# The decay exponents of an SSD scan move from VectorE to ScalarE, and the running sums get another layout in DRAM

## The chip, the cores and the metric

The kernel runs on one core of a Trainium2 chip. The metric is the device time of one execution in microseconds (us). Three executions of the kernel before took 1712.23, 1719.13 and 1721.5 us, so the median is 1719.13 us.

## The reference, cut to what matters

One layer is computed for a prompt of 1024 tokens and for 32 sample rows. It has dilated attention (12 heads), a Mamba-2 SSD scan (16 heads in two groups of 8) beside it, a common output projection and a feed-forward part with a convolution. The change is in the SSD scan of the prompt, which works on 8 chunks of 128 tokens:

```python
acum = jnp.cumsum(dtc * a.reshape(G, hpg), axis=2)
causal = jnp.tril(jnp.ones((q, q), bool))[:, :, None, None]
seg = acum[:, :, :, None] - acum[:, :, None, :]
decay = jnp.exp(jnp.where(causal, seg, -jnp.inf))
cb = jnp.einsum('bcign,bcjgn->bcijg', cc, bc)
y_intra = jnp.einsum('bcijg,bcijgh,bcjghp->bcighp', cb, decay, xdt)
```

`acum` is the running sum of dt * a inside a chunk. `a` is negative, so `seg` is zero or less where the mask is true. The kernel doesn't form minus infinity: it clamps `seg` at zero, takes the exponential, and has the mask in the factor `cb`.

## The kernel before, in words

Every product is made of three float32r products (a high and a low part of each operand). The main stream of TensorE is a list of weight chunks. A chunk has three units of 24 matmuls over 352 tokens each (L1037 to L1039, tile `p_mm`). After a unit its results are taken from PSUM on VectorE, the next chunk's weights are split (`wh` on ScalarE, `wl` on VectorE), and one tick of the side work follows.

The SSD scan is such side work: 16 steps, one for each pair of a group g and a chunk c. A step is a generator, `ssd_gen`, and a tick takes each running step one stage on. The stages are: transposes on TensorE; `xdt` and `cbm`; the decay (`M`, `Ab`, `xdw`); the products M * cbm on VectorE (L1271) and Ab * C on GpSimd (L1272); the matmuls into `p_sa` (L1280 with M, L1285 with Ab, L1287 with xdw); the evacuation on VectorE (`hn`, L1294 or L1296, and `XS`, L1300). `p_sa` has one buffer, so a step's matmuls wait until VectorE has evacuated the step before. For group 0 a new step starts every second tick, for group 1 at every tick. The order on each engine is that in which the program emits the instructions; no engine overtakes its own queue.

For each step the running sums of 8 heads and 128 tokens are loaded from the DRAM scratch `acscr` to all 128 partitions at once (`Ab`, three buffers in rotation; the load for the next step is issued on SyncE's DMA queue, SP, in the stage that takes the present one). In the kernel before `acscr` is stored as 16 heads by 1024 tokens, so a partition's 4 KB come as 8 pieces of 512 bytes. `M` has two buffers.

Of the kernel before, what the change touches and what calls it, by code (L numbers as in the profile page):

```python
# [11 lines left out]
F32 = mybir.dt.float32  # L12
# [7 lines left out]
D = 1024  # L20
S = 1024
# [18 lines left out]
def host_constants():  # L40
    """Arrays that depend on shapes alone: identity, masks and the ALiBi bias of each group."""
    f = np.float32
    c = {}
    i = np.arange(128)
    c["ident"] = np.eye(128, dtype=f)
    c["triu"] = (i[:, None] <= i[None, :]).astype(f)
    h = np.arange(1, NH + 1, dtype=f)
    slopes = np.exp2(f(-8.0) * h / f(NH)).astype(f).reshape(3, 4)
    for g in range(2):
        step = (i[:, None] + 128) - np.arange(256)[None, :]  # L50
        ok = (step >= 0) & (step <= 128)
        b = -slopes[g][None, :, None] * (step * DIL[g]).astype(f)[:, None, :]
        c[f"bias{g}"] = np.where(ok[:, None, :], b, f(NEG)).astype(f)
    step = i[:, None] - i[None, :]
    ok = (step >= 0) & (i[:, None] // 64 == i[None, :] // 64)
    b = -slopes[2][None, :, None] * (step * DIL[2]).astype(f)[:, None, :]
    c["bias2"] = np.where(ok[:, None, :], b, f(NEG)).astype(f)
    bs = np.full((128, 3, 9, 4, 4), NEG, f)
    c16 = i % 16
    for g in range(3):  # L60
        for u in range(U_S[g]):
            for t in range(4):
                if g == 0:
                    step = 128 + t - (9 * c16 + u)
                    ok = (step >= 0) & (step <= 128)
                elif u == U_S[g] - 1:
                    step = 0 * c16
                    ok = c16 == 15
                else:
                    n = U_S[g] - 1  # L70
                    step = 16 * n - n * c16 - u
                    ok = step >= 0
                bb = -slopes[g][None, :] * (step * DIL[g]).astype(f)[:, None]
                bs[:, g, u, t, :] = np.where(ok[:, None], bb, f(NEG))
    c["bias_s"] = bs.reshape(128, 3, 144)
    c["blk16"] = (i[:, None] // 16 == i[None, :] // 16).astype(f)
    c["bsel"] = (i[:, None] // 16 == np.arange(8)[None, :]).astype(f)
    j = np.arange(32)
    same = j[:, None] // 4 == j[None, :] // 4
    btri = (same & (j[:, None] <= j[None, :])).astype(f)  # L80
    pk = np.zeros((128, 256), f)
    pk[:32, 0:32] = btri
    pk[:32, 32:64] = same.astype(f)
    pk[:32, 64:192] = np.tile(btri, (1, 4))
    pk[:, 192:224] = (i[:, None] % 32 == j[None, :]).astype(f)
    for q in range(2):
        pk[:, 224 + q] = (q * 4 + i // 32 == (i % 32) // 4)
    pk[:96, 226:234] = (i[:96, None] % 32 // 4 == np.arange(8)[None, :])
    pk[:16, 234:242] = (np.arange(16)[:, None] // 2 == np.arange(8)[None, :])
    c["pack"] = pk  # L90
    c["par"] = (np.arange(16)[:, None] % 2 == i[None, :] // 64).astype(f)
    return c
# [24 lines left out]
def raw_ap(base, offset, dims):  # L117
# [3 lines left out]
# Buffers in SBUF: shape, type, number in rotation, first and last phase of use. A pair of types makes  # L121
# two views of the same bytes (what a DMA brings, and the rounded part that takes its place).
RAW = (F32, F32R)
BUFFERS = {
    # constants and small things
# [9 lines left out]
    # x, load  # L135
    "xh": ([128, K8, NT], F32R, 1, 0, 6), "xl": ([128, K8, NT], F32R, 1, 0, 6),
    "xt": ([128, D], F32, 4, 0, 0), "jk": ([128, D], F32, 1, 0, 0), "sx": ([128, 4, 128], F32, 2, 0, 0), "xr": ([128, 4, 128], F32, 4, 0, 0), "cst_in": ([128, 3, 128], F32, 1, 1, 1), "cst_g": ([8, 128], F32, 1, 0, 0),
    # q, k, v
# [4 lines left out]
    # attention of the prompt  # L143
# [7 lines left out]
    # attention of the sample rows  # L151
# [5 lines left out]
    # dt  # L157
# [3 lines left out]
    # weights with tokens moving  # L161
    "wl": ([128, D], RAW, 3, 2, 9), "wh": ([128, D], F32R, 2, 2, 9),
    # convolution, SSD, gate
# [12 lines left out]
    # w_out  # L176
# [6 lines left out]
    # feed-forward  # L183
# [6 lines left out]
class Memory:  # L190
    """Places the buffers: those whose phases are apart may share bytes."""
# [22 lines left out]
    @staticmethod  # L214
    def place(items, base, end):
        """Lowest free place for each item in turn; the place of each, or the first that found none."""
        placed, where = [], {}
        for n, (size, name, i, t0, t1) in enumerate(items):
            at = base
            for lo, hi in sorted((o, o + z) for o, z, a, b in placed if not (b < t0 or a > t1)):  # L220
                if at + size <= lo:
                    break
                at = max(at, hi)
            if at + size > end:
                return None, n
            placed.append((at, size, t0, t1))
            where[name, i] = at
        return where, None
# [14 lines left out]
class Side:  # L243
    """Work that runs between the units of the main stream: queues of generators, each advanced a
    stage at a time. A generator that yields True goes on before the next unit's results are taken
    (for what takes the results of its own products), otherwise after."""
# [40 lines left out]
def body(tc, A):  # L287
# [42 lines left out]
    acscr = dr.tile([16, S], F32, name="acscr")  # L330
    acsscr = dr.tile([16, NS], F32, name="acsscr")

# [51 lines left out]
    def rsqrt_mean(dst, src, n, cols):  # L384
        """dst = (src / n + eps) ^ -0.5, on the [P, cols] of both."""
        G.tensor_scalar(dst, src, 1.0 / n, EPS, op0=ALU.mult, op1=ALU.add)
        G.tensor_tensor(dst, dst, neghalf[: dst.shape[0], :cols], op=ALU.pow)
# [14 lines left out]
    def wq_load(sl):  # L402
        """Half slices of w_in for q, k or v of a group, to be split in two parts."""
# [106 lines left out]
    def states_in(sp, dst, nm, rows, per, nf):  # L510
        """A convolution's state of the sample rows, features on partitions."""
# [198 lines left out]
    def att_chain(g, at):  # L710
        """Tiles of a group, four of them under way; a tile's keys stay for the next one."""
        gens = [att_gen(g, i, at) for i in range(8)]
        return gens

# [1 line left out]
    # Partition 16*b + c holds the c-th part of the keys of row b of the batch; every partition does a  # L716
    # softmax of its own part, and the parts of all groups are put together at the end.
# [206 lines left out]
    def dt_gen():  # L924
# [9 lines left out]
        # softplus(x) = max(x, 0) + 2 atanh(e / (2 + e)), e = exp(-|x|)  # L934
# [44 lines left out]
        for q2 in range(2):  # L979
# [6 lines left out]
            SP.dma_start(acscr[:, q2 * 512:(q2 + 1) * 512], aT)  # L986
# [29 lines left out]
    def w_split(n, part, low):  # L1016
        """Half of a weight chunk in two parts: the high one, or the low one."""
# [13 lines left out]
    def fm_unit(ps, hl, moving, c0, k0, k1):  # L1031
        """ps[128 features, CH tokens] += (rows of a weight chunk)^T @ tokens, both in two parts."""
# [15 lines left out]
    def chunk(n, moving, evac, psum=p_mm, after=None, more=None, steps=(0, 2, 2, 2), hold=None, first=0):  # L1048
        """The three units of a weight chunk; the elementwise work of the chunk before runs between them.
        The first rows of all units may go ahead of the others."""  # L1050
# [49 lines left out]
    # ================= q, k, v =================  # L1100
    def group_end(g):
        """What waits for the last tile of a group to be in DRAM."""
# [16 lines left out]
    def samp_rows(g, w):  # L1119
        """What the rows of the sample group of k (w = 1) or v (w = 2) start."""  # L1120
# [52 lines left out]
    # ================= xBC: convolution, SSD =================  # L1173
# [58 lines left out]
    def ab_load():  # L1232
        """The sums of dt * a of the next chunk, the same on every partition."""
        if ab_order:
            g, c = ab_order.pop(0)
            Ab = R("Ab")
            SP.dma_start(Ab, raw_ap(acscr, g * 8 * S + c * 128, [[0, 128], [S, 8], [1, 128]]))
            decays[g, c] = Ab

    def ssd_gen(g, c):  # L1240
# [21 lines left out]
        for h in range(8):  # L1262
            V.tensor_scalar(M[:, h, :], Ab[:, h, :], acum[:, c, g * 8 + h:g * 8 + h + 1], 0.0, op0=ALU.subtract,  # L1263
                            op1=ALU.min)
        AC.activation(M, M, AF.Exp)
# [90 lines left out]
    def samp_ssd():  # L1356
# [5 lines left out]
        # three copies of the tokens, so that a product over 96 rows takes both parts of both operands  # L1362
# [67 lines left out]
        def state(c):  # L1430
            """The states of two heads: what they add to y, decay and new part."""
# [52 lines left out]
    # ================= z: gate =================  # L1484
# [67 lines left out]
    # ================= w_out =================  # L1552
# [6 lines left out]
    def rms_cols(src, dst, scr):  # L1559
        """Per token (sum over features of src / D + eps)^-0.5, the same on every partition of dst."""  # L1560
# [84 lines left out]
    # ================= feed-forward =================  # L1645
# [201 lines left out]
```

## Time and profile before

| | kernel before |
|---|---|
| device time, three executions | 1712.23, 1719.13, 1721.5 us |
| span of the profiled execution | 1718.4 us |
| TensorE (PE) busy | 1627.3 us, 95% |
| VectorE (DVE) busy | 1086.4 us, 63% |
| ScalarE (ACT) busy | 586.2 us, 34% |
| GpSimd (POOL) busy | 406.7 us, 24% |

The span is the time from the first to the last instruction of one profiled execution. The profile gives no separate device time for that execution; its span lies 0.7 us under the median of the three. The shares are means over the whole span, and the stages differ a good deal: the SSD steps lie between 521 and 702 us.

### The profile page before, as it was taken

Reading aid. Unit: us, or ns where it says so; the run is one execution under the profiler, and the core shown is the slowest. Engines: PE = TensorE matmul, PEld = TensorE weight load, DVE = VectorE, ACT = ScalarE, POOL = GpSimd, SP = SyncE. Lnnn points to the kernel's source line nnn. Section 1 sums busy time; section 2 is a strip of 40 time slices with the busy share of each in tenths; the row PEclk is TensorE's granted clock in tenths of the full one; section 3 lists DMA queues with packets and bytes.
Section 4 is the critical chain, followed back from the end, with each engine's and each line's share of the span. In section 5 each row is a group of like instructions: output and inputs, shape, how many; then the busy total and the mean of one; then the engine's idle time right before and its main releaser. Section 6 shows DMA issues by size and latency. Waiting matters only on the chain.

```text
span 1718.4 us, 27938 instructions
## 1 busy us (share of the span) xinstructions
PE 1627.3 (95%) x11167; PEld 1570.2 (91%) x11167; DVE 1086.4 (63%) x1921; ACT 586.2 (34%) x1062; POOL 406.7 (24%) x455
## 2 busy tenths in 40 slices
PE   6988997999998988989999999999999999999998
PEld 6877987889998877889999999999999999999998
DVE  6578877725568898666354555645547456465565
ACT  6424534525734544432232331221221222222121
POOL 6576556400013456531021100000000000000000
PEclk9999998999999998989999999999999999999999
DMA  7543565544355242455211211021120210211102
GB/s 242 145 155 113 168 194 161 148 130 119 79 152 142 59 89 63 143 160 164 66 41 47 92 50 51 25 75 38 37 63 14 75 50 26 63 47 41 51 1 103
DMA packets 193024, 158.16 MB, mean 92 GB/s; under 512 B 18802, under 2 KB 176010, under 8 KB 192895
## 3 DMA queue, kind: packets, MB, share of 16 engines
q1 hardware_dynamic: 192895, 156.38, 31.4%
q8 instruction: 88, 1.44, 0.3%
q14 instruction: 41, 0.34, 0.1%
HBM read 127.63 MB, written 34.68 MB: 94 GB/s over the span
## 4 chain that ended last, share of the span: by engine, by line
PE 75%; DVE 9%; DMA 7%; POOL 3%; issue 3%; ACT 2%; SPq 1%; DVEq 0%; ACTq 0%; POOLq 0%
PE p_up L1037 10%; PE p_up L1039 10%; PE p_up L1038 10%; PE p_mm L1037 6%; PE p_mm L1038 6%; PE p_mm L1039 6%; PE p_dn L1783 5%; PE p_dn L1781 5%; PE p_dn L1782 5%; DMA Ab<-acscr 2%; PE p_mm L554 2%; DVE sq L591 1%; PE p_mm L555 1%; PE p_mm L556 1%; DVE M L1263 1%
## 5 line engine op out<-in xcount | busy, mean ns | idle before, releaser
L1037 PE MATMUL p_up<-x2h,wh 128*128 128x352 f32 x1032 | 334.5, 324 | 0.0
L1039 PE MATMUL p_up<-x2h,wl 128*128 128x352 f32 x1032 | 333.4, 323 | 0.0
L1038 PE MATMUL p_up<-x2l,wh 128*128 128x352 f32 x1032 | 332.9, 323 | 0.0
L1691 DVE TENSOR_TENSOR fci<-p_up,rb 128x352 f32<-128x352 f32 x129 | 66.2, 513 | 238.7 <-PE p_up L1039 237.1
L1037 PEld LDWEIGHTS p_up<-x2h,wh 128*128 128x128 f32 x1032 | 194.1, 188 | 0.2
L1038 PEld LDWEIGHTS p_up<-x2l,wh 128*128 128x128 f32 x1032 | 193.8, 188 | 0.0
L1039 PEld LDWEIGHTS p_up<-x2h,wl 128*128 128x128 f32 x1032 | 193.8, 188 | 0.0
L1785 DVE TENSOR_TENSOR yacc<-yacc,p_dn 128x352 f32<-128x352 f32 x264 | 133.6, 519 | 75.5 <-PE p_dn L1783 75.5
L554 PE MATMUL p_mm<-wqh,xh 128*128 128x256 f32 (+1 forms) x576 | 171.0, 297 | 1.6 <-DVE sb L570 1.6
L1781 PE MATMUL p_dn<-gp,dh 128*128 128x352 f32 x528 | 172.3, 326 | 0.0
L1783 PE MATMUL p_dn<-gp,dl 128*128 128x352 f32 x528 | 171.3, 324 | 0.0
L1782 PE MATMUL p_dn<-gp,dh 128*128 128x352 f32 x528 | 171.0, 324 | 0.0
L556 PE MATMUL p_mm<-wqh,xl 128*128 128x256 f32 (+1 forms) x576 | 165.9, 288 | 0.9 <-POOL xl L461 0.7
L555 PE MATMUL p_mm<-wql,xh 128*128 128x256 f32 (+1 forms) x576 | 165.7, 288 | 0.0
L1037 PE MATMUL p_mm<-xh,wh 128*128 128x352 f32 x480 | 162.5, 338 | 0.0
L1039 PE MATMUL p_mm<-xh,wl 128*128 128x352 f32 x480 | 155.9, 325 | 1.5 <-DVE wl L1027 1.4
L1038 PE MATMUL p_mm<-xl,wh 128*128 128x352 f32 x480 | 156.2, 325 | 0.0
L1029 ACT CAST wh<-wl 128x512 fp32r<-128x512 f32 (+1 forms) x160 | 92.0, 607 | 112.8 <-PE p_up L1038 76.6
L1027 DVE TENSOR_TENSOR wl<-wl,wh 128x512 fp32r<-128x512 f32 (+1 forms) x160 | 120.0, 750 | 3.8 <-ACT wh L1029 3.7
L1709 DVE SCALAR_TENSOR_TENSOR facc<-fci,cw,facc 128x1072 f32<-128x1072 f32 x88 | 116.8, 1327 | 2.1 <-ACT facc L1701 2.0
L554 PEld LDWEIGHTS p_mm<-wqh,xh 128*128 128x128 f32 x576 | 112.5, 195 | 4.9 <-DVE sb L570 1.8
L556 PEld LDWEIGHTS p_mm<-wqh,xl 128*128 128x128 f32 x576 | 112.1, 195 | 1.5 <-POOL xl L461 1.5
(359 smaller groups left out, 3458.0 us busy)
## 6 DMA issues: line engine op xcount, KB each, us to landing
wl<-in_w_up_dram SPq DMA_DIRECT2D x44, 512.0 KB
dl<-in_w_down_dram SPq DMA_DIRECT2D x22, 512.0 KB
kt<-in_cache_kv_dram SPq DMA_DIRECT2D x20, 512.0 KB
wl<-in_w_in_dram SPq DMA_DIRECT2D x20, 512.0 KB
wql<-in_w_in_dram SPq DMA_DIRECT2D x18, 512.0 KB
Ab<-acscr SPq DMA_DIRECT2D x16, 512.0 KB
qscr<-qo SPq DMA_DIRECT2D x48, 128.0 KB
qt<-qscr SPq DMA_DIRECT2D x16, 384.0 KB
```

The source lines that it names most:

```text
L554: T.matmul(ps[:, :n], lhsT=X[0][:, k, c0:c0 + 128], rhs=hi[:, kk, :n], start=k == 0, stop=False)
L555: T.matmul(ps[:, :n], lhsT=X[0][:, k, c0:c0 + 128], rhs=lo[:, kk, :n], start=False, stop=False)
L556: T.matmul(ps[:, :n], lhsT=X[1][:, k, c0:c0 + 128], rhs=hi[:, kk, :n], start=False, stop=k == K8 - 1)
L1027: V.tensor_tensor(lo[:, c], raw[:, c], f32(hi[:, c]), op=ALU.subtract)
L1037: T.matmul(ps[:, :CH], lhsT=hi[:, c], rhs=mh[:, c0:c0 + CH], start=k == 0, stop=False)
L1038: T.matmul(ps[:, :CH], lhsT=hi[:, c], rhs=ml_[:, c0:c0 + CH], start=False, stop=False)
L1039: T.matmul(ps[:, :CH], lhsT=lo[:, c], rhs=mh[:, c0:c0 + CH], start=False, stop=k == len(moving) - 1)
L1709: V.scalar_tensor_tensor(acc[:, :L], ci[:, i:i + L], cw_f[:, i, fu:fu + 1], acc[:, :L], op0=ALU.mult, op1=ALU.add)
L1781: T.matmul(ps[:, :CH], lhsT=hi[:, mc], rhs=GP[:, s2, c], start=x == 0, stop=False)
L1782: T.matmul(ps[:, :CH], lhsT=hi[:, mc], rhs=GP[:, s2 + 1, c], start=False, stop=False)
L1783: T.matmul(ps[:, :CH], lhsT=lo[:, mc], rhs=GP[:, s2, c], start=False, stop=x == len(fs) - 1)
L1785: V.tensor_tensor(yacc[:, m, c], yacc[:, m, c], ps[:, :CH], op=ALU.add)
```

## The change

The eight subtractions with a clamp at zero, min(Ab - acum, 0), one for each head on VectorE, become eight activations on ScalarE, relu(acum - Ab), with `acum` as the bias of each partition and a scale of -1. The exponential that follows takes a scale of -1. The scratch `acscr` is stored as group, chunk, head, token, so that a step's sums are one run of 4 KB. The store that fills it is split: two DMAs in place of one for each half of the tokens. All else in the diff is removed comments.

```diff
-    acscr = dr.tile([16, S], F32, name="acscr")
+    acscr = dr.tile([2, 8, 8, 128], F32, name="acscr")
...
-            SP.dma_start(acscr[:, q2 * 512:(q2 + 1) * 512], aT)
+            for g in range(2):
+                SP.dma_start(acscr[g, q2 * 4:q2 * 4 + 4].rearrange("c h i -> h c i"),
+                             aT[g * 8:g * 8 + 8].rearrange("h (c i) -> h c i", c=4))
...
-            SP.dma_start(Ab, raw_ap(acscr, g * 8 * S + c * 128, [[0, 128], [S, 8], [1, 128]]))
+            SP.dma_start(Ab.rearrange("p h i -> p (h i)"), raw_ap(acscr, (g * 8 + c) * 1024, [[0, 128], [1, 1024]]))
...
         for h in range(8):
-            V.tensor_scalar(M[:, h, :], Ab[:, h, :], acum[:, c, g * 8 + h:g * 8 + h + 1], 0.0, op0=ALU.subtract,
-                            op1=ALU.min)
-        AC.activation(M, M, AF.Exp)
+            AC.activation(M[:, h, :], Ab[:, h, :], AF.Relu, bias=acum[:, c, g * 8 + h:g * 8 + h + 1], scale=-1.0)
+        AC.activation(M, M, AF.Exp, scale=-1.0)
         AC.activation(Ab, Ab, AF.Exp)
```

VectorE's queue at the step (g 1, c 3), before. Names carry a buffer number; `zt` is the gate's chunk, L1492 multiplies it into `XS`:

```order
L1271 TENSOR_TENSOR M_0_212<-M_0_212,cbm_0_220 128x1024
L1263 TENSOR_SCALAR M_0_213<-Ab_0_211,acum_0_69 128x128 x8
L1492 TENSOR_TENSOR XS_0_191<-XS_0_191,zt_0_205 128x1024
L1492 TENSOR_TENSOR XS_0_191<-XS_0_191,zt_0_206 128x1024
L1296 TENSOR_TENSOR hn_0_223<-hn_0_223,p_sa 128x512
L1300 SCALAR_TENSOR_TENSOR XS_0_191<-XS_0_191,dsk_0_76,p_sa 128x128 x4
```

The same place of VectorE's queue after (lines are one or two further on):

```order
L1272 TENSOR_TENSOR M_0_212<-M_0_212,cbm_0_220 128x1024
L1493 TENSOR_TENSOR XS_0_191<-XS_0_191,zt_0_205 128x1024
L1493 TENSOR_TENSOR XS_0_191<-XS_0_191,zt_0_206 128x1024
L1297 TENSOR_TENSOR hn_0_223<-hn_0_223,p_sa 128x512
L1301 SCALAR_TENSOR_TENSOR XS_0_191<-XS_0_191,dsk_0_76,p_sa 128x128 x4
```

The eight clamps of step 3 no longer stand between the product of step 2 and the evacuation of step 1. Nothing else moved on this engine.

ScalarE's queue at the steps (g 1, c 2) and (g 1, c 3), before, with the engines or DMA queues that an instruction waits for:

```order
L1265 ACT_TABLE_LOAD [waits DVE_49]
L1265 ACTIVATE M_0_0_212<-M_0_0_212 128x1024 [waits Activation_49]
L1266 ACTIVATE Ab_1_0_210<-Ab_1_0_210 128x1024 [waits DMAHW4_49,Pool_49]
L1309 COPY ho_0_0_224<-p_st_6394 128x512 [waits DMAHW7_49,DMAHW6_49]
L1257 COPY cbm_2_0_221<-p_st_6424 128x128 [waits DVE_49]
L1265 ACTIVATE M_1_0_213<-M_1_0_213 128x1024 [waits DVE_49,Activation_49]
L1266 ACTIVATE Ab_2_0_211<-Ab_2_0_211 128x1024 [waits DMAHW6_49,Pool_49]
```

The same place after:

```order
L1265 ACTIVATE M_0_0_212<-Ab_1_0_210,acum_0_0_69 128x128 [waits DMAHW6_49,PE_49,Pool_49]
L1265 ACTIVATE M_0_0_212<-Ab_1_0_210,acum_0_0_69 128x128 [waits PE_49] x7
L1266 ACT_TABLE_LOAD
L1266 ACTIVATE M_0_0_212<-M_0_0_212 128x1024 [waits Activation_49]
L1267 ACTIVATE Ab_1_0_210<-Ab_1_0_210 128x1024
L1310 COPY ho_0_0_224<-p_st_6396 128x512 [waits DMAHW1_49,DMAHW0_49]
L1259 COPY cbm_2_0_221<-p_st_6426 128x128 [waits DVE_49]
L1265 ACTIVATE M_1_0_213<-Ab_2_0_211,acum_0_0_69 128x128 [waits DMAHW0_49,PE_49,Pool_49]
L1265 ACTIVATE M_1_0_213<-Ab_2_0_211,acum_0_0_69 128x128 [waits PE_49] x7
L1266 ACTIVATE M_1_0_213<-M_1_0_213 128x1024 [waits Activation_49]
L1267 ACTIVATE Ab_2_0_211<-Ab_2_0_211 128x1024
```

The wait for the load and for TensorE (the matmuls that read the same buffer of M two steps earlier) stands on ScalarE now, and the table load between the relus and the exponential. ScalarE no longer waits for VectorE before the exponential.

## Rows read from the trace of the kernel before

**Rows 1.** The page: span, busy time and share of two engines.

```profile
span 1718.4 us, 27938 instructions
PE 1627.3 (95%) x11167; PEld 1570.2 (91%) x11167; DVE 1086.4 (63%) x1921; ACT 586.2 (34%) x1062; POOL 406.7 (24%) x455
```

**Rows 2.** Busy by stretch: length, PE, PEld, DVE, ACT, POOL, clock, DMA, GB/s.

```profile
612.00:702.00 90.00, 79.56 (x602) 67.97 (x599) 80.03 (x158) 39.74 (x47) 54.87 (x32) 0.93 0.30 67
521.00:702.00 181.00, 159.17 (x1204) 141.03 (x1203) 160.31 (x312) 83.91 (x104) 93.90 (x62) 0.95 0.34 74
```

**Rows 3.** Waits of PE, 521 to 702: total us, times, longest.

```profile
PE p_sa L1280 <- DVE XS L1300: 10.6, 4, 4.1
PE p_sa L1280 <- ACT zt L1496: 5.2, 1, 5.2
PE p_sa L1280 <- issue: 3.3, 1, 3.3
PE p_sa L1280 <- DVE M L1271: 1.7, 2, 1.0
```

**Rows 4.** Timeline of DVE: start, duration, line, tile, shape, count.

```profile
566.27 1.65 DVE L1263 TENSOR_SCALAR M<-Ab,acum 128x128 f32<-128x128 f32 x8
...
602.72 5.39 DVE L1263 TENSOR_SCALAR M<-Ab,acum 128x128 f32<-128x128 f32 x8 [1.81 <-DMA Ab<-acscr]
...
637.19 5.40 DVE L1263 TENSOR_SCALAR M<-Ab,acum 128x128 f32<-128x128 f32 x8
642.51 2.35 DVE L1492 TENSOR_TENSOR XS<-XS,zt 128x1024 f32<-128x1024 f32 x2
...
645.38 1.11 DVE L1300 SCALAR_TENSOR_TENSOR XS<-XS,dsk,p_sa 128x128 f32<-128x128 f32 x4
...
675.77 4.57 DVE L1263 TENSOR_SCALAR M<-Ab,acum 128x128 f32<-128x128 f32 x8
```

**Rows 5.** Groups by line, 521 to 702: busy us, mean ns, idle before.

```profile
L1263 DVE TENSOR_SCALAR M<-Ab,acum 128x128 f32<-128x128 f32 x128 | 45.7, 427 | 6.4 <-DMA Ab<-acscr 3.8 <-issue 2.3
```

**Rows 6.** Timeline of PE: the end of one of these stalls.

```profile
609.88 0.44 PE L1280 MATMUL p_sa<-M,xdt 128*64 128x128 f32 x4 [3.52 <-DVE XS L1300]
```

**Rows 7.** Stretches at the lower clock level: length, PE busy, clock.

```profile
549.70:553.10 3.40, 3.40 (x26) 0.51 0.00 0
...
sum 17.00, PE 15.56; mean PE 3.89
```

**Rows 8.** Timeline of ACT, exponentials of the attention with a bias.

```profile
387.20 0.39 ACT L665 ACTIVATE P<-P,stt 128x128 f32<-128x128 f32 x1
387.49 0.19 ACT L665 ACTIVATION_READ_ACCUMULATOR P<-P,stt 128x1 f32 x1
387.58 0.39 ACT L665 ACTIVATE P<-P,stt 128x128 f32<-128x128 f32 x1
```

**Rows 9.** Groups by line on ACT, whole span: busy us, mean ns, idle.

```profile
L1265 ACT ACTIVATE M<-M 128x1024 f32<-128x1024 f32 x16 | 17.0, 1060 | 50.5 <-DVE M L1263 50.5
...
L1265 ACT ACT_TABLE_LOAD x8 | 10.3, 1283 | 16.8 <-DVE M L1263 10.2 <-issue 6.5
```

**Rows 10.** The chain that ended last: start, us, what.

```profile
248.38 0.45 SPq L986
...
508.42 6.32 DMA F<-fscr
...
577.55 9.71 DMA Ab<-acscr
```

**Rows 11.** Busy by stretch, columns as in rows 2: an `Ab` load, and `rb` with others.

```profile
579.00:583.50 4.50, 4.50 (x32) 4.48 (x32) 3.42 (x8) 3.83 (x5) 3.37 (x4) 1.00 0.47 72
...
944.00:947.00 3.00, 3.00 (x21) 3.00 (x20) 0.00 (x0) 0.62 (x1) 0.00 (x0) 1.00 0.87 266
```

**Rows 12.** A product M * cbm on DVE, and the matmuls that read it.

```profile
683.12 1.21 DVE L1271 TENSOR_TENSOR M<-M,cbm 128x1024 f32<-128x1024 f32 x1
...
690.61 0.37 PE p_sa L1280 x4
```

## The prediction, made before the changed kernel had run

> **What bounds the kernel now.** I read the page first: TensorE is busy 95% of 1718.4 us [rows 1], so only its idle time and its slow stretches can be won. The change lies between 521 and 702 us, where the 16 SSD steps run, so I read that stretch by itself. There TensorE is busy 159.17 of 181 us and VectorE 160.31; ScalarE has 83.91 and GpSimd 93.90 [rows 2]. VectorE is as full as TensorE.
>
> What TensorE waits for is in the waits of the same stretch: 10.6 + 5.2 + 3.3 + 1.7 = 20.8 us in eight stalls, all ahead of L1280, a step's first matmuls [rows 3]. Four of them are put down to `XS` L1300, the end of the evacuation that frees the one `p_sa` buffer. The 5.2 us one is put down to ScalarE, but the timeline of VectorE shows its cause: eight clamps of 5.40 us, two gate products of 2.35 us, then `XS` from 645.38 for 1.11 us, to 646.49 [rows 4]; TensorE goes on at 646.64. So TensorE waits because VectorE, in its fixed order, clamps the decays of later steps before it evacuates the present one.
>
> The stalls have a second price. Four stretches with 17.0 us in all, TensorE busy for 15.56 of them, ran at a granted clock of about 0.5 of full speed, which is 1.2 GHz [rows 7]. They come behind the four longest stalls, of 3.3, 3.5, 4.1 and 5.2 us [rows 3, 6]; the other four, 4.7 us together, have none behind them. At 2.4 GHz the same matmuls take half: 15.56 / 2 = 7.8 us lost. I count with 181 - 20.8 - 7.8 = 152 us as the time that TensorE needs for this stretch.
>
> **The clamps on VectorE** (removed). 128 instructions, 45.7 us, 16 groups, so 2.86 us a group on average [rows 5]. Undisturbed, a group takes 1.65 us, but some take 4.6 to 5.4 [rows 4], and GpSimd is at work during these. I take off all 45.7 us, and 16 x 1.65 = 26.4 us as the low end, since the time lost beside GpSimd may come back on another instruction of VectorE. With them go 3.8 us of waiting for `Ab` loads and 2.3 us marked issue [rows 5], in which the whole queue of VectorE stood still. VectorE then has 115 to 134 us of work for 152.
>
> Stall by stall I compare what VectorE is relieved of just ahead of each. For the four at `XS` these are 1.65 to 7.2 us (5.39 plus a wait of 1.81 at the stall of 3.5 us, 4.57 at that of 4.1, the 1.65 of an undisturbed group at the shortest) against stalls of 4.1 us at most, and for the 5.2 us one 5.40 us [rows 3, 4, 6]: all five go. So do the two at L1271, 1.7 us. Of the 3.3 us one, with no long group ahead of it, I take 2.3 us off, between the undisturbed 1.65 and the mean of 2.86. Sum 10.6 + 5.2 + 1.7 + 2.3 = 19.8 us. No stall of 3.3 us or more is left, so the 7.8 us of the lower clock go too.
>
> **The relus on ScalarE** (added). The trace of before has no relu. The nearest row is an exponential on the same shape with a bias of each partition: 0.39 us, and the next instruction starts 0.29 us later; with the read of its accumulator, which the relus lack, the pair takes 0.38 us from start to start [rows 8]. I take 0.29, with 0.38 as the dear end and 0.20 as the cheap one (VectorE's 1.65 / 8). So a group takes 7 x 0.29 + 0.39 = 2.4 us, and 128 relus take 37 us (26 to 49). ScalarE comes to 84 + 37 = 121 us of 152. The eight table loads of 1.28 us stay eight, but now stand behind the relus, where some ran while ScalarE waited for VectorE [rows 9].
>
> What hides this is idle time of ScalarE that the change itself ends: it waited 50.5 + 10.2 us for the clamps [rows 9]. Behind a relu group in its queue are the exponentials, the copy of `cbm`, the weight casts and the gate's silu and squares; the products on VectorE and GpSimd wait for the exponentials, and TensorE for the products. The tight part is group 1, a step at each unit. There ScalarE has 39.74 us [rows 2] and gets 64 x 0.29 = 19 more, 59 of some 75 us, if I take the stalls and slow clock out of that stretch's 90. Its queue is uneven: at one tick in three come the weight casts, the gate's silu, a square and a table load on top, 3 x 1.06 + 1.28 = 4.5 us if each takes what the exponential of the same width does [rows 9]. Beside an even load such a tick is late by up to two thirds of that, 3 us. The slack for it is larger: a product ended at 684.33 and its matmuls began at 690.61 [rows 12], 6.3 us later. If that cover were gone, five such ticks would cost 15 us. I take 2 us, near the end of nothing, because of this slack.
>
> **The load of `Ab`** (reshaped). Now 512 KB take 9.71 us from issue to the next link of the chain [rows 10], and move at 72 GB/s [rows 11]. The nearest load after the change's form is `rb`, one run of 4,224 bytes to each partition; with the weights beside it 266 GB/s were moved [rows 11]. At 72 GB/s 512 KB take 7.3 us, so 2.4 of the 9.71 us are start and landing; at 266 GB/s they take 2.0, and 2.0 + 2.4 = 4.4 us, which I take. The dear end is 6.32 us, for `F`, whose loads give every partition a 4 KB run while stores run beside them [rows 10]. Nothing beyond the stalls counted above waits for `Ab`, so I add nothing; if the load stayed at 9.71 us, ScalarE would take over the wait of 3.8 us [rows 5].
>
> On the load, the row says that pieces of 512 bytes run at 72 GB/s here. The Trainium skill (DMA: Bandwidth & Descriptors, Specifications) puts the smallest transfer for line rate at 512 bytes. By that rule the new layout changes nothing in the load; this case's trace disagrees for this load, at least with the rule as the whole story.
>
> **The split store.** Two more DMAs on SP at about 248 and 251 us. One such issue takes 0.45 us and lies on the chain [rows 10], ahead of a key load and a bias load in the queue. I add 0.4 us; 0 and 0.9 are its ends.
>
> **Sum.** -19.8 - 7.8 + 2.0 + 0.4 = -25.2 us, so the span goes from 1718.4 to 1693.2. The span lies 0.7 us under the median of the three runs, 1719.13, so I forecast 1694 us.
>
> **Rivals.** *The stalls come back at another wait.* GpSimd has 54.87 us in the second half of the steps [rows 2], of some 75 then. If the 19 us which the clamps lost beside GpSimd (45.7 - 26.4) fall on the evacuation, or the ticks with the gate's work are late by the whole 15 us above, about half of the 25 us comes back: 1694 + 13 = 1707. For it: the M product, undisturbed 1.2 us [rows 12], stands on both sides of that contention. Against it: VectorE has room, 134 of 152 us.
>
> *The end of the stretch is set elsewhere.* TensorE would then reach the work behind 702 us earlier and wait there for loads and casts: 1719, within 0.5%. Against it: nothing of that work is due by a clock; it is emitted behind the same units, and its loads are issued there too.
>
> *A longer chain, slower.* If the clamp's own length sets the end, each undisturbed group grows from 1.65 to 2.4 us, 16 x 0.75 = 12 us: 1731. It decides only if the matmuls wait for M itself, not for `XS`, that is if the clamps' mean of 2.86 us were below 2.4. Only 1.7 of 20.8 us are put down to M now [rows 3].
>
> The last rival is also what the Trainium skill (ScalarE: Activation LUTs, Rules for kernel authors) would lead to: it gives relu, min and max to VectorE, which it calls faster per element. On rows of this case it is right for an undisturbed group, 1.65 against an estimated 2.4 us, and not for the mean group of 2.86 us.
>
> **How the numbers follow.** The forecast has 0.63, the first rival 0.19, the second 0.12, the third 0.06. With 0.5% (8.6 us, about what a measurement of this kernel can tell from no change) as the bound, the first two are faster, 0.82; then 0.12 the same and 0.06 slower. The likeliest case reaches from 1687 (every stall and the whole clock loss gone, nothing added: 1719 - 28.6 = 1690, and 3 us less for the spread of the runs) to 1702 (8 us of new stalls). With the first rival's 1707 and a few us above it the range is 1685 to 1711, and leaves out about two in ten.
>
> **What would show it.** On VectorE no clamps are left, and it is busy 115 to 134 us in the steps' stretch, which shrinks to 150 to 158 us. On ScalarE stand 128 activations of about 0.39 us, 0.29 apart, and no wait for VectorE ahead of the exponentials. The waits of TensorE at L1280 fall from 20.8 to under 5 us, and no stretch there has the lower clock. `Ab` lands 4 to 5 us after its issue. The prediction is wrong if TensorE's waits at L1280 stay but name ScalarE or GpSimd, if a relu takes over 0.6 us, or if the wait moves behind 702 us.

## The result and the profile after

Four executions of the changed kernel took 1697.16 to 1701.62 us, median 1698.19. The kernel before had a median of 1716.8 us in four. The ratio is 0.990, with a 95% interval of 0.9881 to 0.992, so the change saves about 17 us (14 to 20). The forecast was 1694 us, in a range of 1685 to 1711.

The page after, as in [rows 1]:

```profile
span 1695.8 us, 27926 instructions
PE 1619.7 (96%) x11167; PEld 1565.7 (92%) x11167; DVE 1047.9 (62%) x1793; ACT 624.7 (37%) x1190; POOL 403.1 (24%) x455
```

The steps' stretch began at 521 us before and begins at 520.5 now (just ahead of the first `Ab` load); it ended at 702 and ends at 681.5 (last `XS`). Busy by stretch, columns as in [rows 2]; the second row is a short stretch inside, at the lower clock:

```profile
520.50:681.50 161.00, 152.65 (x1205) 137.17 (x1204) 122.37 (x184) 122.31 (x232) 92.15 (x62) 0.99 0.27 83
...
654.40:657.80 3.40, 3.40 (x29) 2.78 (x26) 0.75 (x1) 2.48 (x7) 3.40 (x3) 0.51 0.00 0
```

The stretch is 20.0 us shorter, out of 22.6 for the span. VectorE fell from 160.31 of 181 us to 122.37 of 161, ScalarE rose from 83.91 to 122.31. The lower clock is left in one stretch (0.51 of full speed, 1.2 GHz); its 3.4 us would take half at 2.4 GHz, so by this estimate 1.7 us are lost to it, where it was 7.8.

The waits of TensorE in that stretch, as in [rows 3]:

```profile
PE p_sa L1281 <- DVE XS L1301: 3.5, 2, 1.8
PE p_sa L1286 <- POOL Ab L1273: 2.5, 1, 2.5
PE p_sa L1281 <- issue: 1.4, 1, 1.4
PE p_st L1251 <- DVE xdt L1255: 1.0, 1, 1.0
```

These are 8.4 us, where it was 20.8. What VectorE did ahead of the two evacuations `XS` that TensorE waited for is in its timeline:

```profile
620.08 3.26 DVE L1272 TENSOR_TENSOR M<-M,cbm 128x1024 f32<-128x1024 f32 x1
623.26 3.19 DVE L1493 TENSOR_TENSOR XS<-XS,zt 128x1024 f32<-128x1024 f32 x2
...
632.44 3.41 DVE L1493 TENSOR_TENSOR XS<-XS,zt 128x1024 f32<-128x1024 f32 x1
```

A product with `cbm` took 3.26 us, where an undisturbed one took 1.21 [rows 12], and one gate product took 3.41 us. By line, the 16 products with `cbm` (busy us, mean ns, idle):

```profile
L1272 DVE TENSOR_TENSOR M<-M,cbm 128x1024 f32<-128x1024 f32 x16 | 30.0, 1873 | 0.0
```

GpSimd worked beside both long ones, in its own timeline:

```profile
619.90 2.36 POOL L1273 TENSOR_TENSOR Ab<-Ab,BC 128x1024 f32<-128x1024 f32 x1 [0.67 <-ACT Ab L1267]
...
631.40 3.37 POOL L1273 TENSOR_TENSOR Ab<-Ab,BC 128x1024 f32<-128x1024 f32 x1
```

ScalarE's timeline in two steps:

```profile
525.12 2.45 ACT L1265 ACTIVATE M<-Ab,acum 128x128 f32<-128x128 f32 x8 [0.66 <-POOL xdw L1269]
...
582.68 2.45 ACT L1265 ACTIVATE M<-Ab,acum 128x128 f32<-128x128 f32 x8 [0.38 <-DMA Ab<-acscr]
```

Its line L1265, durations as min/median/max in ns:

```profile
L1265 ACT ACTIVATE M<-Ab,acum x128: 383/387/410, 525.1 to 666.9; 128x128 f32<-128x128 f32 x128
```

The only wait of the relus for a load in the steps:

```profile
ACT M L1265 <- DMA Ab<-acscr: 0.4, 1, 0.4
```

A group of eight relus takes 2.45 us, and no relu took over 0.41 us, whatever GpSimd did. The load that the second group waited for was issued here, in SyncE's timeline:

```profile
578.02 0.55 SPq L1239 DMA_DIRECT2D Ab<-acscr  x1
```

It was waited for until 582.68, so this load landed at most 4.7 us after its issue, against 9.71 [rows 10]. The relus waited for no other load, so this is the only one that the trace dates.

The stall of 2.5 us is a piece of the chain that ended last (start, us, what; lines between are left out):

```profile
638.48 1.14 ACT wh L1031 x2
639.62 1.28 ACT L1514
640.92 1.09 ACT zt L1514
642.00 2.34 ACT M L1265 x8
644.36 1.28 ACT L1266
645.66 1.06 ACT M L1266
...
651.27 2.81 POOL Ab L1273
```

Directly ahead of that product, GpSimd's own timeline has another instruction, the addition of the gate's squares (`ssq`):

```profile
648.75 2.55 POOL L1498 TENSOR_TENSOR ssq<-ssq,zt 128x1024 f32<-128x1024 f32 x1 [3.42 <-ACT cbm L1259]
```

One tick with the weight casts and the gate's silu on ScalarE puts two table loads (1.28 us), the relus and the exponentials in a row. GpSimd then adds the gate's squares, 2.55 us, and only then starts the product; the stall is as long as that addition.

### The profile page after: what moved, and what is told of

Same layout as the page of the kernel before. It is cut to its first block, busy times and chain, and to the rows that moved or that the text cites. A ratio compares the mean times of both kernels' runs of the same rounds, so it can differ in the third digit from the quotient of the medians.

```text
span 1695.8 us, 27926 instructions
## 1 busy us (share of the span) xinstructions
PE 1619.7 (96%) x11167; PEld 1565.7 (92%) x11167; DVE 1047.9 (62%) x1793; ACT 624.7 (37%) x1190; POOL 403.1 (24%) x455
## 4 chain that ended last, share of the span: by engine, by line
PE 78%; DVE 8%; DMA 4%; POOL 4%; ACT 3%; issue 2%; SPq 1%; DVEq 0%; POOLq 0%; ACTq 0%
PE p_up L1039 10%; PE p_up L1041 10%; PE p_up L1040 10%; PE p_mm L1039 7%; PE p_mm L1040 7%; PE p_mm L1041 7%; PE p_dn L1784 5%; PE p_dn L1782 5%; PE p_dn L1783 5%; DVE sq L591 2%; PE p_mm L554 1%; PE p_mm L555 1%; PE p_mm L556 1%; POOL sm L387 1%; DMA qt<-qscr 1%
```

## The experiments

The theory after the result: **A**, VectorE's full queue made the evacuation of `p_sa` late, and relief of it is the gain. Its rivals: **B**, the slow load of `Ab` was what held up the steps, so that the new layout is the gain; **C**, the chain clamp, exponential, product got shorter by the move. All runs of one series share the runs of the kernel before; its median was 1716.8 us in the changed kernel's series and 1714.5, 1718.3, 1716.6 and 1718.1 us in the four later ones, so the ratios are what is compared.

| run | median us | ratio to before, 95% interval |
|---|---|---|
| changed kernel | 1698.19 | 0.9900 (0.9881 to 0.9920) |
| relus alone | 1699.76 | 0.9912 (0.9895 to 0.9929) |
| layout alone | 1711.93 | 0.9982 (0.9970 to 0.9994) |
| changed + 8 clamps a step | 1720.94 | 1.0038 (1.0025 to 1.0051) |
| changed + 8 relus a step | 1720.18 | 1.0033 (1.0019 to 1.0048) |
| changed + 4 clamps a step | 1706.21 | 0.9935 (0.9917 to 0.9953) |
| changed + 4 relus a step | 1704.09 | 0.9922 (0.9904 to 0.9940) |
| four heads clamped, four by relu | 1709.07 | 0.9945 (0.9925 to 0.9966) |
| gate products spread | 1698.29 | 0.9891 (0.9872 to 0.9909) |
| before, no Ab * C product | 1695.20 | 0.9884 (0.9861 to 0.9906) |
| changed, no Ab * C product | 1690.25 | 0.9848 (0.9827 to 0.9870) |
| changed, Ab * C on VectorE | 1693.05 | 0.9859 (0.9839 to 0.9879) |
| changed, Ab * C in halves | 1692.04 | 0.9855 (0.9834 to 0.9875) |

### The two parts of the change alone

The relus with the old layout and the one store:

```diff
-    acscr = dr.tile([2, 8, 8, 128], F32, name="acscr")
+    acscr = dr.tile([16, S], F32, name="acscr")
...
-            SP.dma_start(Ab.rearrange("p h i -> p (h i)"), raw_ap(acscr, (g * 8 + c) * 1024, [[0, 128], [1, 1024]]))
+            SP.dma_start(Ab, raw_ap(acscr, g * 8 * S + c * 128, [[0, 128], [S, 8], [1, 128]]))
```

> The clamps go to ScalarE, the layout of the sums in DRAM stays as before (512-byte pieces, 9.7 us a load). Theory A (VectorE's full queue made TensorE wait): nearly the whole gain of 19 us is here; the 3.8 us that VectorE waited for loads moves to ScalarE, so 1698 to 1703 us, stalls of TensorE ahead of its first matmuls of a step 5 to 10 us. Theory B (the slow load made TensorE wait): half of the gain or less, 1707 us or more. Theory C (the chain clamp, exponential, product sets the pace): not faster than the full change, and ScalarE waits for the load at most steps.

The new layout with the clamps on VectorE:

```diff
-            AC.activation(M[:, h, :], Ab[:, h, :], AF.Relu, bias=acum[:, c, g * 8 + h:g * 8 + h + 1], scale=-1.0)
-        AC.activation(M, M, AF.Exp, scale=-1.0)
+            V.tensor_scalar(M[:, h, :], Ab[:, h, :], acum[:, c, g * 8 + h:g * 8 + h + 1], 0.0, op0=ALU.subtract,
+                            op1=ALU.min)
+        AC.activation(M, M, AF.Exp)
```

> The clamps stay on VectorE, the sums of a step lie as one 4 KB run. Theory A: only the 6.1 us in which VectorE's queue stood still go, so 2 to 6 us faster than before, 1711 to 1715 us, and the stalls of TensorE before a step's first matmuls stay at 15 us or more of 20.8. Theory B: most of the gain is here, 1698 to 1705 us.

The relus alone give 0.9912, nearly the whole gain, and the layout alone 0.9982. B falls. The layout shortens the load without being the bound: with the old one ScalarE takes over the wait of 3.8 us that VectorE had [rows 5], and more, and the time is not told apart from the changed kernel's (2 us more, with an interval of some 4 us either way). This is ScalarE's wait in the run with the relus alone:

```profile
ACT M L1263 <- DMA Ab<-acscr: 9.9, 5, 3.7
```

### Work put back on either engine

Eight clamps a step into a tile `dum` that nobody reads, on VectorE, or eight relus on ScalarE (`ident` is a constant):

```diff
+            V.tensor_scalar(dum, ident, acum[:, c, g * 8 + h:g * 8 + h + 1], 0.0, op0=ALU.subtract, op1=ALU.min)
```

> The full change, and at the place of the old clamps VectorE does eight clamps of the same shape from a constant tile into a tile that nobody reads (additional work, the output is the reference's). Theory A: the time goes back up by 8 to 16 us, to 1706 to 1714 us, with the stalls before a step's first matmuls put down to the evacuation again, though nothing waits for these clamps. Theory C: within 3 us of the full change, since the chain of a step is as in the full change.

```diff
+        for h in range(8):
+            AC.activation(dum, ident, AF.Relu, bias=acum[:, c, g * 8 + h:g * 8 + h + 1], scale=-1.0)
```

> The full change with eight more relus a step on ScalarE, ahead of the real ones, from a constant tile into a tile that nobody reads (additional work, the output is the reference's). ScalarE goes from 122 to about 160 us in the steps' stretch, which is 161 us long. If the slack of 6 us ahead of the matmuls hides ScalarE's work as the prediction had it, the first few us a step are free in the half with a step at every second unit, and the half with a step at each unit becomes bound: 8 steps x about 2 us, so 1706 to 1716 us. If the relus lie on the chain that sets the pace already (theory C): 16 x 2.4 = 38 us, 1736 us.

Then half as many of each:

> The changed kernel with 4 clamps a step on VectorE into a tile that nobody reads (64 instructions, by the run with 8 some 20 to 22 us). VectorE then has 122 + 21 = 143 of some 161 us. Theory A with a knee (what costs is a queue so full that the evacuation of p_sa comes late): there is room, most of the 43 us of the run with 8 did its harm above that, so 2 to 8 us over the changed kernel, 1700 to 1706 us on the chip where the kernel before takes 1717. Rival D (each us on VectorE ahead of the evacuation costs in proportion, 22 us / 43 us = 0.5): 11 us, 1709. XS is named in the waits of TensorE either way.

> The changed kernel with 4 relus a step on ScalarE into a tile that nobody reads (64 instructions of 0.3 to 0.39 us, some 20 us). ScalarE then has 122 + 20 = 142 of some 161 us. With a knee: 0 to 5 us over the changed kernel, since ScalarE's lateness still lies inside the slack ahead of the matmuls, 1698 to 1703 us. In proportion (22 us for 8 relus): 11 us, 1709, with stalls at XS and at the product on GpSimd.

The windows from 520 to 690 us, columns as in [rows 2]. Eight clamps added, then the two longest waits of TensorE:

```profile
520.00:690.00 170.00, 145.49 (x1082) 128.17 (x1080) 158.21 (x292) 115.20 (x226) 81.32 (x54) 0.95 0.22 69
```

```profile
PE p_sa L1283 <- DVE XS L1303: 13.8, 4, 6.1
PE p_sa L1283 <- DVE M L1274: 3.8, 2, 2.8
```

Eight relus added, and its two longest waits of TensorE:

```profile
520.00:690.00 170.00, 145.73 (x1080) 128.66 (x1079) 100.03 (x162) 159.55 (x342) 78.26 (x54) 0.93 0.22 70
```

```profile
PE p_sa L1284 <- DVE XS L1304: 10.0, 2, 7.0
PE p_sa L1289 <- POOL Ab L1276: 9.5, 4, 4.9
```

Four clamps added:

```profile
520.00:690.00 170.00, 155.17 (x1201) 138.58 (x1200) 147.73 (x246) 121.92 (x232) 91.64 (x59) 0.97 0.24 73
```

Four relus added:

```profile
520.00:690.00 170.00, 158.06 (x1214) 141.57 (x1213) 113.81 (x182) 145.35 (x297) 91.44 (x59) 0.96 0.24 73
```

No step waits for the result of the added clamps, yet they cost the whole gain and more, and TensorE's waits name `XS`, the evacuation, at 13.8 us, and the product `M`, which stands behind the clamps in the same queue, at 3.8: C falls as the main cause. Of 1717 us the added four clamps cost 0.0035, or 6 us, the second four 0.0103, or 18 us; the relus 4 and 19 us. The costs of the first four have an interval of some 5 us either way, those of the second four some 4 us. So there is a knee: at 145 to 148 of 170 us of work an engine costs little, at 158 to 160 it becomes the bound. (With eight added, the steps are not over at 690 us, so these two shares leave out the end of the steps.) A holds, and the same goes for ScalarE, which the change has filled to 122 of 161. Both sizes at eight were missed on the low side: I expected 1706 to 1714 for the clamps and 1706 to 1716 for the relus.

Four heads stay on VectorE, with two exponentials of half the width:

```diff
-        for h in range(8):
+        for h in range(4, 8):
+            V.tensor_scalar(M[:, h, :], Ab[:, h, :], acum[:, c, g * 8 + h:g * 8 + h + 1], 0.0, op0=ALU.subtract,
+                            op1=ALU.min)
+        for h in range(4):
             AC.activation(M[:, h, :], Ab[:, h, :], AF.Relu, bias=acum[:, c, g * 8 + h:g * 8 + h + 1], scale=-1.0)
-        AC.activation(M, M, AF.Exp, scale=-1.0)
+        AC.activation(M[:, :4, :], M[:, :4, :], AF.Exp, scale=-1.0)
+        AC.activation(M[:, 4:, :], M[:, 4:, :], AF.Exp)
```

> Four of a step's eight heads are clamped on VectorE (new layout), four by relus on ScalarE, and the exponential becomes two of half the width. VectorE gets back 13 to 23 us (122 + 18 = 140 of 161), ScalarE loses 18 to 20 and gains the fixed part of one more exponential a step. If VectorE's queue alone is what counts, with a knee: within 4 us of the changed kernel, and with part of the cost of the 4 refilled clamps, 1699 to 1704; in proportion: half of the gain is lost, 1707 to 1709. If ScalarE's length of 2.4 us a group still costs something in the changed kernel, this one is faster than it: 1693 to 1697.

It keeps 0.0055 of the 0.010, as proportion would have it, and not the 1699 to 1704 us that I expected from a knee. Its window, with VectorE as full as with four added clamps and ScalarE at 106.54:

```profile
520.00:690.00 170.00, 155.97 (x1212) 139.59 (x1211) 147.82 (x245) 106.54 (x185) 94.74 (x62) 0.98 0.26 82
```

It lies 8 us (interval some 5 either way) over the changed kernel, so "little" at this share is 4 to 8 us, and below it a cost in proportion is not excluded; the knee rests on the second four. Its clamps, grouped by line as in [rows 5]:

```profile
L1265 DVE TENSOR_SCALAR M<-Ab,acum 128x128 f32<-128x128 f32 x64 | 29.5, 520 | 0.0
```

Half the clamps take 29.5 us, not half of 45.7: their mean rises from 427 ns [rows 5] to 520. What makes them long does not halve with their number, and that led to the last four runs.

### What the long instructions of VectorE wait for

The gate adds one product a tick in place of two:

```diff
-                side.add("yg", [yg_step(f, z)], 2)
+                side.add("yg", [yg_step(f, z)], 1)
```

> The changed kernel with one stage of the gate's product a tick in place of two, so that the two products of 1.6 us of the gate (L1493) do not stand in one piece between the product with cbm and the evacuation on VectorE. What is left of the stalls at p_sa in the changed kernel is 8.4 us, of which 3.5 us name XS behind these products. If they are the cause, these 3.5 us and part of the 1.7 us of the lower clock go: 0 to 4 us faster than the changed kernel, 1694 to 1698. If the products only come later in a tick that is as full: no difference, 1698 plus or minus 2.

The waits for `XS` go from 3.5 to 1.1 us, as the first case expected, and the time stays. The gain is given back behind the steps, from 681 to 760 us, where TensorE waits for the low parts of the first tiles of the output projection (`A0l`, `A1l`, from the attention). The longest of these waits, first in the changed kernel, then in this one:

```profile
PE p_mm L1040 <- POOL A0l L1533: 2.6, 1, 2.6
```

```profile
PE p_mm L1040 <- POOL A0l L1533: 7.5, 1, 7.5
```

In all, 6.1 us there (2.6 + 2.5 + 1.0) become 9.6 (7.5 + 1.5 + 0.6). These tiles do not need the gate's products; they stand behind them in GpSimd's queue. GpSimd's timeline, again the changed kernel first:

```profile
703.21 3.29 POOL L1498 TENSOR_TENSOR ssq<-ssq,zt 128x1024 f32<-128x1024 f32 x1 [5.81 <-ACT zt L1497]
706.46 3.43 POOL L1533 TENSOR_TENSOR A0l<-A0l,A0h 128x1056 fp32r<-128x1056 f32 x1
```

```profile
704.82 6.37 POOL L1498 TENSOR_TENSOR ssq<-ssq,zt 128x1024 f32<-128x1024 f32 x1 [5.81 <-ACT zt L1497]
711.15 3.40 POOL L1533 TENSOR_TENSOR A0l<-A0l,A0h 128x1056 fp32r<-128x1056 f32 x1
```

The addition of the gate's squares starts 1.6 us later and takes 6.37 us in place of 3.29, and the subtraction that makes `A0l` starts 4.7 us later for it. What made that one addition so long is not shown.

The next two leave out GpSimd's product of Ab and C (so Ab goes to the matmuls without the factor C), once from the kernel before and once from the changed one:

```diff
-        G.tensor_tensor(Ab, Ab, Ct[:, None, :].to_broadcast([128, 8, 128]), op=ALU.mult)
```

> The kernel before, with GpSimd's product of Ab and C left out in each step (16 instructions of 2.2 to 3.4 us; Ab goes to the matmuls without the factor C, which changes the result). If the long clamps are long because GpSimd works beside them, their sum falls from 45.7 us toward 16 undisturbed groups, 26.4 us: I expect 28 to 36 us, and with VectorE relieved by 12 to 20 us the time falls by 6 to 14 us, to 1703 to 1711 where the kernel before takes 1717. If their length has another cause, the clamps stay at 44 to 47 us, and the time falls by 3 us at most.

> The changed kernel with the same product of GpSimd left out. What is left of the stalls there is 8.4 us and 1.7 us of lower clock: 2.5 us of it name this product, and 3.5 us stand behind a product with cbm of 3.26 us and gate products of 3.2 to 3.4 us on VectorE. If both come of GpSimd's work, the product with cbm falls from 30.0 us in 16 toward 16 x 1.2 = 19 us and the time by 4 to 9 us against the changed kernel, to 1690 to 1695. If only the wait for GpSimd itself goes: 2 to 4 us, 1695 to 1697. The gap to the run of the kernel before without the product tells how much of the change's gain was relief from GpSimd's contention: with it gone on both sides I expect the gap to fall from 18 to 10 to 14 us.

The kernel before, without the product: clamps and products with `cbm` by line, then the clamps' durations (min/median/max, ns), then TensorE's longest wait.

```profile
L1263 DVE TENSOR_SCALAR M<-Ab,acum 128x128 f32<-128x128 f32 x128 | 34.3, 339 | 8.5 <-DMA Ab<-acscr 6.1 <-issue 2.4
L1271 DVE TENSOR_TENSOR M<-M,cbm 128x1024 f32<-128x1024 f32 x16 | 22.0, 1375 | 0.1
```

```profile
L1263 DVE TENSOR_SCALAR M<-Ab,acum x128: 273/277/1165, 529.2 to 665.0; 128x128 f32<-128x128 f32 x128
```

```profile
PE p_sa L1279 <- DVE XS L1299: 4.4, 4, 1.4
```

In the kernel before as it was: the products by line, the clamps and the evacuation by duration, and from GpSimd's timeline the product that ran inside the 5.40 us group of [rows 4].

```profile
L1271 DVE TENSOR_TENSOR M<-M,cbm 128x1024 f32<-128x1024 f32 x16 | 27.3, 1703 | 0.1
```

```profile
L1263 DVE TENSOR_SCALAR M<-Ab,acum x128: 270/277/2436, 529.7 to 685.6; 128x128 f32<-128x128 f32 x128
...
L1300 DVE SCALAR_TENSOR_TENSOR XS<-XS,dsk,p_sa x64: 330/340/344, 541.8 to 701.8; 128x128 f32<-128x128 f32 x64
```

```profile
638.14 2.39 POOL L1272 TENSOR_TENSOR Ab<-Ab,BC 128x1024 f32<-128x1024 f32 x1
```

The same clamp of 277 ns in the median took up to 2,436 ns before and at most 1,165 without the product. 2.44 us is what GpSimd's product takes (2.39): the clamp stands still for the length of a whole product. (Two other instructions of GpSimd in each step, `hn` and `xdw`, take 1.18 and 1.25 us in the mean in the run without the product. That would fit the 1,165 ns, but no run leaves them out.) Without GpSimd's product the clamps take 11.4 us less and the products with `cbm` 5.3, TensorE's waits for `XS` fall from 10.6 to 4.4, and the kernel before becomes as fast as the changed one: 0.9884, 20 us. I had expected 6 to 14; the mechanism was right and the size too small. Leaving the product out also takes its own 2.4 us off the way to TensorE's matmuls, but in the kernel before TensorE hardly waited for it:

```profile
PE p_sa L1285 <- POOL Ab L1272: 0.3, 1, 0.3
```

The changed kernel without the product has next to no stall left in the steps; its window and its only wait from 515 to 685 us:

```profile
520.00:690.00 170.00, 169.03 (x1323) 153.84 (x1322) 112.55 (x200) 127.52 (x241) 52.62 (x49) 1.00 0.32 100
```

```profile
PE p_st L1251 <- DVE xdt L1255: 1.0, 1, 1.0
```

Here, with that disturbance gone on both sides, the change is worth 0.0036, or 6 us (interval some 5 either way), not 17; I expected 10 to 14. Next to no stall is left to remove, so the 6 us are what the run before it had left to gain.

The experiments point to a version, and the last two runs are it. The product goes to VectorE, or half of it:

```diff
-        G.tensor_tensor(Ab, Ab, Ct[:, None, :].to_broadcast([128, 8, 128]), op=ALU.mult)
+        V.tensor_tensor(Ab, Ab, Ct[:, None, :].to_broadcast([128, 8, 128]), op=ALU.mult)
```

> The changed kernel with the product of Ab and C on VectorE in place of GpSimd; the whole result is computed. The run that left this product out took 1690 us with no stall in the steps, and VectorE had 112.6 of 170 us there; 16 products at the 1.37 us that the product of the same shape took in that run add 22 us, some 135 of 165. If what counts is how long VectorE's queue is with GpSimd's disturbance gone: there is room, and the product's 2.4 to 3.4 us on GpSimd leave the chain to the matmuls, so 1691 to 1697 us, 1 to 7 faster than the changed kernel. If each us on VectorE costs as in the run with 4 refilled clamps (35 us for 6 us): 4 us of the 8 are lost, 1694. If the order of the queue counts (the product now stands ahead of the evacuation): 1700 to 1706.

```diff
-        G.tensor_tensor(Ab, Ab, Ct[:, None, :].to_broadcast([128, 8, 128]), op=ALU.mult)
+        V.tensor_tensor(Ab[:, :4, :], Ab[:, :4, :], Ct[:, None, :].to_broadcast([128, 4, 128]), op=ALU.mult)
+        G.tensor_tensor(Ab[:, 4:, :], Ab[:, 4:, :], Ct[:, None, :].to_broadcast([128, 4, 128]), op=ALU.mult)
```

> The changed kernel with four heads of the product of Ab and C on VectorE and four on GpSimd; the whole result is computed. Both engines end the product earlier (0.7 us on VectorE, 1.2 us on GpSimd undisturbed), but they work beside each other. If the disturbance by GpSimd goes with its busy time, about half of the 8 us between the changed kernel and the run without the product: 1693 to 1697. If the halves disturb each other as long as the whole did: 1697 to 1701.

With the whole product on VectorE, the window and the longest wait for `p_sa`:

```profile
520.00:690.00 170.00, 166.03 (x1301) 150.20 (x1300) 131.62 (x215) 125.99 (x239) 53.45 (x47) 1.00 0.30 95
```

```profile
PE p_sa L1281 <- DVE XS L1301: 2.1, 3, 0.9
```

With half of it on either engine:

```profile
520.00:690.00 170.00, 165.35 (x1295) 149.66 (x1295) 133.17 (x215) 127.22 (x240) 78.76 (x62) 1.00 0.30 95
```

Both beat both kernels, at 0.9859 and 0.9855, some 7 us (interval some 5 either way) under the changed kernel's 0.9900; the two are not told apart, and the halves did a little better than the half of the 8 us that I expected. With the whole product VectorE takes on 16 products (22.5 us), yet its busy time is lower than with four added clamps (131.62 against 147.73): those 64 clamps took 34.9 us, and the products with `cbm` take 20.5 us here against 26.3 there, since they are disturbed less. The kernel before with the product on VectorE was not run, so what moving the blocker alone is worth stays open.

## Why the prediction was right, step by step

The forecast of 1694 us is 4 us under the measured 1698.19, well inside its range. The direction and the mechanism (VectorE's queue, relieved) are what the runs showed; the two terms for the stalls and the lower clock were too large. Of the signs named ahead, the stretch came to 161 us and not to 150 to 158, and one stretch kept the lower clock; the waits at L1281 (L1280 before) are 4.9 us, just under the 5 named, but 3.5 us more stand at L1286 and L1251.

**The stalls, -19.8.** They fell by 12.4 (20.8 to 8.4). I left 1.0 us of them; 5.9 are left that do not name GpSimd's product. The step that was too large was "all five go", drawn from comparing each stall with the clamps just ahead of it, with all 45.7 us taken off. VectorE's busy time in the whole span fell by 38.5 (1086.4 to 1047.9): 7.2 of the clamps' 45.7 us came back on other instructions, such as the products with `cbm`, 27.3 to 30.0 us. That is the first rival's mechanism, at a little over a third of its 19 us.

**The lower clock, -7.8.** 6.1 came true. The 1.7 us left stand behind the one stall of 2.5 us, which I had not counted.

**ScalarE's lateness, +2.0.** A relu group was estimated at 2.4 us and took 2.45, a relu 0.39, ScalarE at 121 of 152 and came to 122 of 161. The lateness is one stall of 2.5 us, where the chain runs through the weight casts, the silu, the relus, a table load, the exponentials and GpSimd's addition of the gate's squares before GpSimd's product can start: the uneven tick that I described, with a link on GpSimd that I had left out. But the cover has an end: 64 more relus cost 4 us, 128 cost 23.

**The load.** 4.4 us was taken; at most 4.7 was seen for the one load that was waited for, and by the run with the relus alone nothing large hung on it. The 512 bytes that the Trainium skill names as the smallest transfer for line rate (DMA: Bandwidth & Descriptors, Specifications) do not carry over to this load: the same 512 KB took 9.71 us in pieces of 512 bytes and at most 4.7 in runs of 4 KB. **The split store, +0.4,** shows nowhere in the sum.

**The sum.** -25.2, with 4.9 for stalls that stayed, 0.5 for ScalarE's stall and 1.7 for its clock, less the 0.4 of the store, is -18.5. The stretch lost 20.0. Of the 1.5 between them, 1.0 are three waits of 0.3 to 0.4 us that my 20.8 left out (TensorE's idle time in the stretch was 181 - 159.17 = 21.8 us); 0.5 I cannot assign. 2.6 of the span's 22.6 lie outside the steps, 0.5 ahead of and 2.1 behind them. The profiled execution took 1697.85 us for a span of 1695.8, so 2.05 us lie around a span, not the 0.7 that I read off the median. By that the traced execution of the kernel before took an estimated 1720.4 us, 3.6 over its median of 1716.8, so the traces show more gain than the medians: 22.6 us against 18.6, and 17 by the ratio. The 25 us of the forecast are a third to a half too large against those two, and that its time is off by only 4 us is in part luck: the median that I started from, 1719.13, lay 2.3 us above that of all four.

**The rivals.** The stalls came back in part, as told. The end of the stretch was not set elsewhere: the work behind 702 us moved up with it (1718.4 - 702 = 1016.4 us from there to the end before, 1695.8 - 681.5 = 1014.3 after). A longer chain did not decide: a relu group is longer than an undisturbed clamp group, 2.45 against 1.65 us, and the relus alone still gave 0.9912. The rule of the Trainium skill (ScalarE: Activation LUTs, Rules for kernel authors), relu on VectorE, agrees with those two durations and not with the time, since it does not ask which engine is full. (The prediction gives its reason as faster per element; the page puts that for bf16, and the tiles here are float32.)

What I did not see is how much of the gain hung on GpSimd. I read the 19 us that the clamps lost as theirs, to be removed with them. The runs show that most of them are the disturbance's: without GpSimd's product 11.4 us of them are gone with every clamp still in place, and leaving that product out of the kernel before gives as much as the change. The two loads add up to a full queue, and taking off either one brings it under the knee: VectorE has 139.82 of 170 us in that run, and 126.07 with the change. The Trainium skill (SBUF — State Buffer, Who interferes with whom) has the rule for it: VectorE and GpSimd share a port pair, which whoever comes first holds for a whole instruction; a VectorE instruction with two inputs in SBUF, or one in a mode with two ports, contends, one with at most one SBUF input outside such a mode doesn't. This case's traces fit that: the clamp that took 2.44 us against a product of 2.39 (it has one input in SBUF, so by the rule it ran in a mode with two ports, which no trace here shows), the products with `cbm` (two SBUF inputs) from 1.2 to 3.4 us, and the evacuation `XS` (one input from PSUM) at 330 to 344 ns in 64 of 64. The same section says that ScalarE waits on no other engine for SBUF, and the 128 relus at 383 to 410 ns agree.

## What to carry to other kernels

Before an elementwise operation is moved, compare its shortest and its mean duration: a mean well above the median (here 427 and 277 ns, with one of 2,436) was the sign that another engine blocked it, and easing the blocker was worth as much as easing the blocked. Read an engine's load as a share of the stretch, not of the span: extra work cost 4 to 8 us up to 148 of 170 us, and 18 to 19 us for the next portion of the same number of instructions. A stall that is removed at one place should be looked for at whatever stands behind the moved work in its queues, as with the gate's products: TensorE's waits in the steps fell by 3.5 us, and those behind the steps rose by 3.5.

## What the runs showed of the hardware that was not expected

A single VectorE clamp of 128x128 floats stood still for 2.44 us beside one GpSimd product, nine times its median of 0.277; without that product the same 128 clamps took 34.3 us in place of 45.7. Half as many clamps, beside the same product, took 29.5 us: the loss did not halve with the number of clamps. A load of 512 KB to 128 partitions took at most 4.7 us in runs of 4 KB, where another took 9.71 in pieces of 512 bytes.
